# Eight positions modulo 256 bytes for the split-weight buffers of a two-layer decoder trunk

## The chip, the cores and the metric

The kernel runs on one core of one Trainium2 chip. The metric is the device time of one execution in microseconds. Five engines of the core take part: TensorE (PE; its weight loads are shown apart as PEld), VectorE (DVE), ScalarE (ACT), GpSimd (POOL) and SyncE (SP), which here issues DMAs.

## The reference

A sequence of 256 tokens of width 2048 goes through two layers. Layer 0 mixes tokens with a Conformer convolution module, layer 1 with causal stick-breaking attention of 16 heads; each is followed by a gated feed-forward part with 5632 channels and a depthwise convolution of width 3. In short, with all data in float32:

```python
for i in range(2):
    shift, scale, gate = ada_ln(c, mix_mod_w[i], mix_mod_b[i])
    h = rms_norm(x, mix_norm_g[i]) * (1.0 + scale) + shift
    y = conformer_conv_module(h, ...) if i == 0 else stick_breaking_mixer(h, qkv_w, o_w)
    x = x + gate * y
    shift, scale, gate = ada_ln(c, ffn_mod_w[i], ffn_mod_b[i])
    h = rms_norm(x, ffn_norm_g[i]) * (1.0 + scale) + shift
    x = x + gate * conv_ffn(h, up_w[i], dw_w[i], dw_b[i], down_w[i])
return rms_norm(x, final_norm_g)
```

The convolution module is `h @ pw1`, a gate, a causal depthwise convolution of width 31, layer norm, silu, `@ pw2`. `ada_ln` multiplies the conditioning vector by a matrix of 2048 x 6144.

## The kernel before

Activations lie transposed: 128 channels on the partitions, 256 tokens along a row, so that a width of 2048 is 16 tiles. All weights are cut into blocks of 128 x 128 and packed on the host, in the order of use, into pieces of eight blocks (128 x 1024 float32, 4096 bytes in each partition). The order of products is pw1, pw2, then up and down in two halves, q/k/v by groups of heads, o, and up and down again.

The products (all but pw1) are computed with split operands. A piece arrives by DMA in one of six `raw` buffers. ScalarE rounds it to fp32r, which gives `wh` (line 244), and VectorE subtracts, which gives `wl` (line 248). Activations are split in the same way into a hi and a lo tile: `hh`/`hl` after a norm, `zh`/`zl` into pw2, `gh`/`gl` into down, `oh`/`ol` into o. For each block, `gemm` issues a triple of matmuls that add into one PSUM tile:

```python
nc.tensor.matmul(o, wh[:, c], xh[kt], ...)   # L298: hi tile past wh
nc.tensor.matmul(o, wh[:, c], xl[kt], ...)   # L299: lo tile past wh
nc.tensor.matmul(o, wl[:, c], xh[kt], ...)   # L300: hi tile past wl
```

The weight block is loaded into the array and the activation tile of 256 columns moves past it. In the v product (lines 1131 to 1133) the roles are swapped: the activations are the loaded weights, and 512 columns of `wh` or `wl` move. pw1 (line 664) runs in plain float32 on `raw`, without a split. Line 577 multiplies rows of the modulation matrices ("row matmuls"); its data come in the tiles `mrow`, `mraw`, `zrow` and, for three tiles at the end of the convolution, in the split-weight buffers.

Where the tiles lie: the pool `wsplit` has four `wh` and four `wl` buffers of 4096 bytes. 4096 is 16 x 256, so all eight begin at one position modulo 256. Blocks in a piece are 512 bytes apart and keep that position. Tiles of activations take 1056 bytes each (`hh` and `hl` by their 258 columns, the others because `skewed` gives them 8 columns more), and hi and lo alternate, so each begins 32 bytes further on modulo 256 than the one before: hi tiles have four positions, each lo tile is 32 bytes past its hi tile, and the eight positions are all taken.

The convolution of the first stage reads its gated inputs from `u` tiles; tile j lies in buffer j modulo `UBUFS`. A loop over rounds c = 0 to 16 spreads the taps of tile c over rounds c and c + 1. Tiles 0 to 7 are gated up to round 0; tiles 8 to 14 are gated in rounds 2, 4, 6, 8, 9, 11 and 13, and tile 15 in round 14.

The order of instructions on each engine comes from the program's order and, outside some stretches that `in_order` fixes, from a scheduler that looks at readiness and buffers. Engines run their queues strictly in that order. A split of a piece waits until TensorE has done with the piece four before, since that one has the buffers.

Of the kernel before, what the change touches and what calls it, by code (L numbers as in the profile page):

```python
# [10 lines left out]
F32 = mybir.dt.float32  # L11
F32R = mybir.dt.float32r
# [4 lines left out]
P = 128  # L17
PB = 8
PW = PB * P
# [7 lines left out]

SKEW = {"z": (1, 1), "g0": (1, 1), "g1": (1, 1), "o": (1, 1)}
HEAD = 16
UBUFS = 9  # L30
M0 = 6
MORE_ROWS = 4
SPLIT_ROWS = 3
# [84 lines left out]
def hybrid_trunk(ctx: ExitStack, tc: tile.TileContext, cfg: Cfg, io: dict):  # L118
# [7 lines left out]
    xpool = ctx.enter_context(tc.tile_pool(name="xpool", bufs=1))  # L126
    hpool = ctx.enter_context(tc.tile_pool(name="hpool", bufs=1))
    raw_pool = ctx.enter_context(tc.tile_pool(name="raw", bufs=6))
    w_pool = ctx.enter_context(tc.tile_pool(name="wsplit", bufs=4))
    tmp = ctx.enter_context(tc.tile_pool(name="tmp", bufs=2))  # L130
    mpool = ctx.enter_context(tc.tile_pool(name="mpool", bufs=3))
    acc = ctx.enter_context(tc.tile_pool(name="acc", bufs=5, space=PSUM))
# [92 lines left out]
    def load(src, dst):  # L225
        tc.keep_in_program_order(nc.sync.dma_start(dst, src))

    def load_next():
# [4 lines left out]
        load(io["w_" + name][i, :, :n], v[:, :n])  # L233
        raws.append((blocks, v, n))

    def split_next(later=False):

        blocks, v, n = raws[len(parts)]
        if stream[len(parts)][0] == "pw1":
            parts.append((blocks, v, None))  # L240
            return
        wh = w_pool.tile([P, PW], F32R, name="wh")
        wl = w_pool.tile([P, PW], F32R, name="wl")
        nc.scalar.copy(wh[:, :n], v[:, :n])  # L244
        parts.append((blocks, wh, wl))

        def low():
            nc.vector.tensor_tensor(wl[:, :n], v[:, :n], wh[:, :n].bitcast(F32), op=ALU.subtract)  # L248

        if later:  # L250
            return low
        low()
# [243 lines left out]
    with ExitStack() as cv:  # L496
# [39 lines left out]
        def load_rows(most=1):  # L536

            while row_chunks and most:
                n = nrow["n"]
                near = n < nrow["near"]  # L540
                home = row_homes[n] if near else ("zmm"[n % 3] if n < 8 * KD // 4 else "zm"[n % 2]) if "z" in cpar else "m"
                cap = {"m": 3 if near else 1 + (n < 8 * KD // 4), "r": MORE_ROWS, "w": SPLIT_ROWS, "z": 1}[home]
                if sum(t[1] == home for t in row_tiles) >= cap:
                    break
                m, c, k0 = row_chunks.pop(0)
                src = io["mr_" + m][mr_at[m].index(c), :, k0 * 512:(k0 + 4) * 512]
                if home == "w":
                    v = [w_pool.tile([P, PW], F32R, name=x).bitcast(F32) for x in ("wh", "wl")]
                    for i in range(2):
                        load(src[:, i * PW:(i + 1) * PW], v[i])  # L550
                    v = [v[g // 2][:, g % 2 * 512:(g % 2 + 1) * 512] for g in range(4)]
                else:
                    v = (cpool2.tile([P, 4 * 512], F32, name="mrow", bufs=MORE_ROWS) if home == "r" else
                         cpar["z"].tile([P, 4 * 512], F32, name="zrow") if home == "z" else
                         mpool.tile([P, 4 * 512], F32, name="mraw"))
                    if "z" in cpar:
                        nc.gpsimd.dma_start(v, src)
                    else:
                        load(src, v)
                    v = [v[:, g * 512:(g + 1) * 512] for g in range(4)]  # L560
                row_tiles.append((v, home))
                nrow["n"] += 1
                most -= 1
# [80 lines left out]
        PADW = CW - 1  # L644
        us = [cpool2.tile([P, PADW + T], F32, name=f"u{i}") for i in range(UBUFS)]
        for u in us:
# [25 lines left out]
        def gate_mul(j, sg):  # L672
            nc.vector.scalar_tensor_tensor(us[j % UBUFS][:, PADW:], banks.pop(j)[:, :T], pc("pw1_b", j, 1), sg,
                                           op0=ALU.add, op1=ALU.mult)
# [9 lines left out]
        def conv_first(j):  # L684
            if len(conv_banks) < 2:
                conv_banks.append(psum_b())
            conv_ps[j] = conv_banks[j % 2][:, j // 2 % 2 * T:(j // 2 % 2 + 1) * T]
            nc.scalar.activation(conv_ps[j], us[j % UBUFS][:, PADW:], AF.Identity, bias=pc("cdb", j, 1),  # L688
                                 scale=tap(j, PADW))
# [5 lines left out]
        def conv_tensor(j):  # L695

            tens_ps[j] = psum_acc()[:, :T]
            for i in range(LATE_PE):
                k = PADW - LATE_PE + i
                nc.tensor.matmul(tens_ps[j], diag.pop((j, i)), us[j % UBUFS][:, k:k + T], start=i == 0,  # L700
                                 stop=i == LATE_PE - 1)

        def conv_tap(j, k):
            nc.vector.scalar_tensor_tensor(conv_ps[j], us[j % UBUFS][:, k:k + T], tap(j, k), conv_ps[j],  # L704
                                           op0=ALU.mult, op1=ALU.add)
# [3 lines left out]
        def conv_prod(j, i):  # L709
            v = spare.pop(0) if spare else hpool.tile([P, T + 2], F32R, name=f"hl{len(prods) % PRODUCTS}")  # L710
            prods.append(v)
            pr = v[:, :T].bitcast(F32)
            nc.scalar.activation(pr, us[j % UBUFS][:, i:i + T], AF.Copy, scale=tap(j, i))  # L713
            return pr
# [103 lines left out]
        for c in range(KD + 1):  # L818
            late = gates_at.get(c, [])
            squared, squares = [(j, y_square(j)) for j in squares], []  # L820
            if c < M0 + 6:
                load_rows()
            split = lambda j: len(vector_taps(j)) - len(vector_taps(j)) // 2
            taps = [(c, k) for k in vector_taps(c)[:split(c)]] if c < KD else []
            if c > 0:
                old = [(c - 1, k) for k in vector_taps(c - 1)[split(c - 1):]]
                n = max(len(taps), len(old))
                pad = lambda v: v + [None] * (n - len(v))
                taps = [t for pair in zip(pad(taps), pad(old)) for t in pair if t]
            made = 0  # L830
            for s in range(nd):
# [17 lines left out]
                if c == KD and s == 0:  # L849
                    low = split_next(later=True)  # L850
# [322 lines left out]
    for h in range(2):  # L1173
        t = slice(h * HT, (h + 1) * HT)
        nc.vector.reciprocal(rs[:, t], std[:, t])
        v = mpool.tile([P, D], F32, name="mraw")[:, :KD * HT].rearrange("p (k t) -> p k t", k=KD)
# [129 lines left out]
```

## Time and profile before

| | |
|---|---|
| Time, median of 2 runs | 2307.89 us (2307.41 to 2308.37) |
| Span of the profiled execution, first to last instruction | 2304.7 us |
| Mean granted TensorE clock | 0.997 |
| Matmul instructions shown / on lines 298 to 300 | 17834 / 15744 |
| HBM read | 598.58 MB |

The profiled execution's own time is its span and some microseconds around it that no instruction fills; the median of the runs stands 3.2 us above the span. A row of a group in the profile reads: line, engine, operation, tile written <- tiles read, shape, number; then busy time in us, mean ns of one; then the engine's idle time before these. A row of instructions on a tile has the minimum, median and maximum of their durations in ns. A matmul's duration is partly modelled and overlaps the next one's, so its rate is read from how many start in a stretch.

### The profile page before, as it was taken

How to read it: one execution, taken by the hardware profiler on the slowest of the kernel's cores; microseconds unless marked ns; L12 is line 12 of the kernel's file. 1: busy time of each engine (PE TensorE's matmuls, PEld its weight loads, DVE VectorE, ACT ScalarE, POOL GpSimd, SP SyncE). 2: the span in 40 equal slices, each digit the busy share in tenths (PEclk: the TensorE clock that was granted, in tenths of full speed). 3: DMA queues.
4: the chain of work that ended last, by engine and by line, in shares of the span. 5: the costliest groups of instructions: out<-in, count | busy, mean ns of one | idle time of the engine just before them, and what ended most of it. 6: DMA issues, size and time to landing. Idle time of an engine off the chain costs nothing.

```text
span 2304.7 us, 44243 instructions
## 1 busy us (share of the span) xinstructions
PE 2270.8 (99%) x17834; PEld 2168.1 (94%) x17834; DVE 1736.7 (75%) x2386; ACT 1164.4 (51%) x1776; POOL 334.6 (15%) x478
## 2 busy tenths in 40 slices
PE   7999999999999999999999999999999999999997
PEld 5888678999999999999999999999999999999997
DVE  7689968899998899999975555668666545666654
ACT  2056655755543355554465555657555434555443
POOL 4058713200000000002111000121000000000010
PEclk9999999999999999999999999999999999999999
DMA  9988799789999999999854555555555555555553
GB/s 397 417 328 306 272 368 355 272 320 356 358 347 384 363 345 361 355 350 345 304 189 159 165 173 167 172 190 179 190 187 189 187 188 186 190 189 187 190 185 110
DMA packets 139167, 603.56 MB, mean 262 GB/s; under 512 B 15441, under 2 KB 15569, under 8 KB 115153
## 3 DMA queue, kind: packets, MB, share of 16 engines
q1 hardware_dynamic: 120242, 464.42, 56.0%
q0 software_dynamic: 18720, 136.32, 15.8%
q8 instruction: 139, 2.28, 0.4%
q14 instruction: 66, 0.54, 0.1%
HBM read 598.58 MB, written 2.10 MB: 261 GB/s over the span
## 4 chain that ended last, share of the span: by engine, by line
PE 88%; DVE 5%; DMA 4%; ACT 1%; issue 1%; POOL 0%; DVEq 0%; SPq 0%; POOLq 0%; ACTq 0%
PE ps L298 25%; PE ps L299 25%; PE ps L300 25%; PE ps L664 5%; DMA mraw<-in_mt_mix 3%; DVE mraw L331 2%; DVE wl L248 1%; PE ps L1133 1%; PE ps L1131 1%; PE ps L1132 1%; DMA mraw<-in_mt_ffn 1%; PE ps L577 1%; PE auxa L577 1%; DVE hl L382 0%; PE auxb L1132 0%
## 5 line engine op out<-in xcount | busy, mean ns | idle before, releaser
L248 DVE TENSOR_TENSOR wl<-raw,wh 128x1024 fp32r<-128x1024 f32 x688 | 842.9, 1229 | 412.7 <-ACT wh L244 408.0
L244 ACT CAST wh<-raw 128x1024 fp32r<-128x1024 f32 x688 | 719.5, 1048 | 823.9 <-PE ps L299 642.1
L298 PE MATMUL ps<-hh,wh 128*128 128x256 f32 (+1 forms) x3264 | 915.8, 281 | 0.0
L299 PE MATMUL ps<-hl,wh 128*128 128x256 f32 (+1 forms) x3264 | 912.1, 279 | 0.0
L300 PE MATMUL ps<-hh,wl 128*128 128x256 f32 (+1 forms) x3264 | 908.3, 278 | 0.1
L299 PEld LDWEIGHTS ps<-hl,wh 128*128 128x128 f32 x3264 | 617.7, 189 | 0.3
L300 PEld LDWEIGHTS ps<-hh,wl 128*128 128x128 f32 x3264 | 612.8, 188 | 0.7 <-DVE wl L248 0.7
L298 PEld LDWEIGHTS ps<-hh,wh 128*128 128x128 f32 x3264 | 612.7, 188 | 0.3
L299 PE MATMUL ps<-gl,wh 128*128 128x256 f32 x1408 | 396.0, 281 | 0.0
L300 PE MATMUL ps<-gh,wl 128*128 128x256 f32 x1408 | 393.7, 280 | 2.1 <-DVE wl L248 2.1
L298 PE MATMUL ps<-gh,wh 128*128 128x256 f32 x1408 | 394.9, 280 | 0.0
L331 DVE CUSTOM_DVE_ANT_0 mraw<-mraw,csr 128x2048 f32<-128x2048 f32 x152 | 348.2, 2292 | 46.3 <-DMA mraw<-in_mt_mix 30.2
L300 PEld LDWEIGHTS ps<-gh,wl 128*128 128x128 f32 x1408 | 265.5, 189 | 2.3 <-DVE wl L248 2.3
L299 PEld LDWEIGHTS ps<-gl,wh 128*128 128x128 f32 x1408 | 266.5, 189 | 0.0
L298 PEld LDWEIGHTS ps<-gh,wh 128*128 128x128 f32 x1408 | 265.6, 189 | 0.0
L397 POOL TENSOR_TENSOR sumsq<-sumsq,t 128x256 f32<-128x256 f32 x56 | 66.2, 1183 | 879.8 <-ACT t L393 879.5
L664 PE MATMUL ps<-hh,raw 128*128 128x256 f32 x832 | 188.8, 382 | 0.0
L664 PEld LDWEIGHTS ps<-hh,raw 128*128 128x128 f32 x832 | 157.8, 191 | 28.3 <-issue 5.8
L967 DVE SCALAR_TENSOR_TENSOR t<-ps,par,t 128x254 f32<-128x254 f32 x328 | 157.3, 480 | 3.9
L704 DVE SCALAR_TENSOR_TENSOR auxb<-u,cpar,auxb 128x256 f32<-128x256 f32 x297 | 121.6, 483 | 4.5 <-ACT auxb L688 3.7
L839 POOL TENSOR_TENSOR y<-y,hl 128x256 f32<-128x256 f32 x143 | 104.4, 730 | 13.4 <-ACT hl L713 3.3
L964 ACT ACTIVATE t<-ps,par 128x256 f32<-128x256 f32 x164 | 91.9, 560 | 0.0
(247 smaller groups left out, 2270.5 us busy)
## 6 DMA issues: line engine op xcount, KB each, us to landing
raw<-in_w_down SPq DMA_DIRECT2D x176, 512.0 KB, 4.5
mraw<-in_mt_ffn POOLq DMA_DIRECT2D x64, 1024.0 KB, 8.3
raw<-in_w_pw SPq DMA_DIRECT2D x96, 512.0 KB, 8.0
mraw<-in_mt_mix POOLq DMA_DIRECT2D x48, 1024.0 KB, 8.2
raw<-in_w_up01b SPq DMA_DIRECT2D x84, 512.0 KB, 7.0
raw<-in_w_up11b SPq DMA_DIRECT2D x84, 512.0 KB, 3.5
raw<-in_w_up00b SPq DMA_DIRECT2D x80, 512.0 KB, 7.6
raw<-in_w_up10b SPq DMA_DIRECT2D x80, 512.0 KB, 3.5
```

Source lines behind the costliest of these rows:

```text
L244: nc.scalar.copy(wh[:, :n], v[:, :n])
L248: nc.vector.tensor_tensor(wl[:, :n], v[:, :n], wh[:, :n].bitcast(F32), op=ALU.subtract)
L298: nc.tensor.matmul(o, wh[:, c], xh[kt], start=first, stop=False, skip_group_check=halves > 0)
L299: nc.tensor.matmul(o, wh[:, c], xl[kt], start=False, stop=False, skip_group_check=halves > 0)
L300: nc.tensor.matmul(o, wl[:, c], xh[kt], start=False, stop=left[nb] == 0, skip_group_check=halves > 0)
L331: nc.vector.tensor_tensor_reduce(out=v, in0=v, in1=csr, scale=1.0, scalar=0.0, op0=ALU.mult, op1=ALU.add, accum_out=macc[:, nb:nb + 1])
L397: engine.tensor_tensor(self.sum, self.sum, sq, op=ALU.add)
L664: nc.tensor.matmul(banks[j][:, nb // KD * T:(nb // KD + 1) * T], w[:, b * P:(b + 1) * P], hf[kt], start=first, stop=left[j] == 0, skip_gro ...
L704: nc.vector.scalar_tensor_tensor(conv_ps[j], us[j % UBUFS][:, k:k + T], tap(j, k), conv_ps[j], op0=ALU.mult, op1=ALU.add)
L839: nc.gpsimd.tensor_tensor(ys[c], ys[c], pr, op=ALU.add)
L964: nc.scalar.activation(y, ps[:, :T], AF.Identity, bias=pc(f"fdb{i}", nb, 1), scale=w(FW - 1))
L967: nc.vector.scalar_tensor_tensor(y[:, s:], ps[:, :T - s], w(k), y[:, s:], op0=ALU.mult, op1=ALU.add)
```

## The change

The pool `wsplit` now has one buffer for each of eight names, `wh0`, `wl0`, ... `wh3`, `wl3`, and each gets some columns more: by the second number of its pair in `W_PHASES`, eight float32 (32 bytes) each. The first number, an offset in the tile, is 0 everywhere. A counter takes the four pairs in turn, for the splits and for the row tiles as before. The padding is 3, 1, 2, 7, 4, 6, 3 and 0 times 32 bytes in the order wh0, wl0, wh1, ..., so in units of 32 bytes modulo 256 the eight begin at 0, 3, 4, 6, 5, 1, 7 and 2: the `wh` at 0, 4, 5, 7 and the `wl` at 3, 6, 1, 2. The padding is 832 bytes in each partition, and everything allocated behind the pool moves by as much. One `u` buffer of 1152 bytes goes.

```diff
-UBUFS = 9
+UBUFS = 8
+W_PHASES = [((0, 3), (0, 1)), ((0, 2), (0, 7)), ((0, 4), (0, 6)), ((0, 3), (0, 0))]
...
-    w_pool = ctx.enter_context(tc.tile_pool(name="wsplit", bufs=4))
+    w_pool = ctx.enter_context(tc.tile_pool(name="wsplit", bufs=1))
...
+    turn_of = {"w": 0}
+
+    def w_tiles():
+
+        i = turn_of["w"]
+        turn_of["w"] = (i + 1) % len(W_PHASES)
+        return [w_pool.tile([P, PW + 8 * pad], F32R, name=f"{x}{i}")[:, 8 * at:8 * at + PW]
+                for x, (at, pad) in zip(("wh", "wl"), W_PHASES[i])]
+
     def split_next(later=False):
...
-        wh = w_pool.tile([P, PW], F32R, name="wh")
-        wl = w_pool.tile([P, PW], F32R, name="wl")
+        wh, wl = w_tiles()
         nc.scalar.copy(wh[:, :n], v[:, :n])
...
                 if home == "w":
-                    v = [w_pool.tile([P, PW], F32R, name=x).bitcast(F32) for x in ("wh", "wl")]
+                    v = [x.bitcast(F32) for x in w_tiles()]
```

The numbers of instructions stay the same but for one memset of a `u` buffer. Their order changes in a few places, since the scheduler now sees eight names of one buffer and not two of four. The place that the prediction speaks of is the entry of pw2, where layer norm makes the z tiles one by one. On ScalarE, from the first z tile on, there stood before (L925 is the activation that makes z, L378 its hi part, L244 the weight cast):

```order
L378 CAST zh_2259<-t 128x256
L244 CAST wh<-raw 128x1024
L925 ACTIVATE t<-t,cpar 128x256
L378 CAST zh_2271<-t 128x256
L244 CAST wh<-raw 128x1024
L925 ACTIVATE t<-t,cpar 128x256
L378 CAST zh_2283<-t 128x256
L925 ACTIVATE t<-t,cpar 128x256
L378 CAST zh_2291<-t 128x256
L244 CAST wh<-raw 128x1024 x4
```

After, with lines moved by nine, and with a number behind `wh` that rises in the program's order (2293 is the fourth piece of pw2, 2433 the fifth, 2471 the sixth):

```order
L387 CAST zh_2257<-t 128x256
L253 CAST wh_2261<-raw 128x1024
L934 ACTIVATE t<-t,cpar 128x256
L387 CAST zh_2269<-t 128x256
L253 CAST wh_2273<-raw 128x1024
L253 CAST wh_2433<-raw 128x1024
L253 CAST wh_2471<-raw 128x1024
L934 ACTIVATE t<-t,cpar 128x256
L387 CAST zh_2281<-t 128x256
L934 ACTIVATE t<-t,cpar 128x256
L387 CAST zh_2289<-t 128x256
L253 CAST wh_2293<-raw 128x1024
```

The fifth and sixth cast now stand ahead of the third z tile (zh_2281; it was zh_2283), and the fourth behind the fourth z tile as before. On VectorE, between the second and third zl (y and t lead to the next z tile), before:

```order
L379 TENSOR_TENSOR zl_2272<-t,zh_2271 128x256
L599 TENSOR_TENSOR v_mix_98<-auxb,cpar 128x4x4
L522 TENSOR_TENSOR gb<-v_mix_98,cpar 128x16
L248 TENSOR_TENSOR wl<-raw,wh 128x1024
L923 TENSOR_TENSOR y_191<-y_191,dm 128x256
L924 TENSOR_TENSOR t<-y_191,rstd 128x256
L379 TENSOR_TENSOR zl_2284<-t,zh_2283 128x256
```

And after:

```order
L388 TENSOR_TENSOR zl_2270<-t,zh_2269 128x256
L608 TENSOR_TENSOR v_mix_98<-auxb,cpar 128x4x4
L531 TENSOR_TENSOR gb<-v_mix_98,cpar 128x16
L257 TENSOR_TENSOR wl_2274<-raw,wh_2273 128x1024
L932 TENSOR_TENSOR y_191<-y_191,dm 128x256
L257 TENSOR_TENSOR wl_2434<-raw,wh_2433 128x1024
L933 TENSOR_TENSOR t<-y_191,rstd 128x256
L257 TENSOR_TENSOR wl_2472<-raw,wh_2471 128x1024
L388 TENSOR_TENSOR zl_2282<-t,zh_2281 128x256
```

The subtractions of the fifth and sixth piece moved with their casts. On TensorE, at the end of the second piece of pw2 (tile zh_2271), before:

```order
L299 MATMUL ps<-zl_2272,wh 128x256
L300 MATMUL ps<-zh_2271,wl 128x256
L577 MATMUL ps<-mraw,hot 32x512 x4
L298 MATMUL ps<-zh_2283,wh 128x256
L299 MATMUL ps<-zl_2284,wh 128x256
```

And after:

```order
L308 MATMUL ps<-zl_2270,wh_2261 128x256
L309 MATMUL ps<-zh_2269,wl_2262 128x256
L586 MATMUL ps<-mraw,hot 32x512 x8
L307 MATMUL ps<-zh_2281,wh_2273 128x256 x4
L308 MATMUL ps<-zl_2282,wh_2273 128x256
```

Four row matmuls more stand ahead of the third piece; the last of the eight reads the row tile after the next. They are missing further on, between the fifth and the sixth piece. SyncE's queue is unchanged.

## The prediction

> **What bounds the kernel now.** First the page: the busy times and the granted clock.
>
> ```profile
> span 2304.7 us, 44243 instructions
> PE 2270.8 (99%) x17834; PEld 2168.1 (94%) x17834; DVE 1736.7 (75%) x2386; ACT 1164.4 (51%) x1776; POOL 334.6 (15%) x478
> PEclk9999999999999999999999999999999999999999
> ```
>
> TensorE is busy in 99% of the span at an undisturbed clock. Since ends of matmuls are modelled, busy time alone says little, so next I count matmuls in windows by stage (columns: stretch, its length, then busy time and number of instructions of each engine, clock, DMA share, GB/s).
>
> ```profile
> 440.00:1050.00 610.00, 609.60 (x5214) 609.39 (x5213) 575.43 (x710) 302.86 (x410) 50.28 (x95) 1.00 0.94 355
> 1582.00:2290.00 708.00, 708.00 (x6055) 708.00 (x6054) 429.39 (x542) 345.20 (x454) 13.35 (x14) 1.00 0.56 184
> ```
>
> A count takes in the two or three matmuls in flight at an edge (one is shown as 279 ns, and one starts about every 117 ns: 2.4). So the pace, from start to start, is 610.00 / (5214 - 2.4) = 117.05 ns in the first stretch, and 708.00 / (6055 - 2.4) = 116.97 ns in the second. Between them DMA falls from 94% to 56% and VectorE from 94% to 61%, and the pace doesn't move. So neither feeds the limit: it is TensorE's own pace, **117.0 ns a matmul**, and the change is worth what it does to this number. The count comes from the page and from the instructions that touch wl:
>
> ```profile
> L300 PE MATMUL ps<-hh,wl 128*128 128x256 f32 (+1 forms) x3264 | 908.3, 278 | 0.1
> L300 PE MATMUL ps<-gh,wl 128*128 128x256 f32 x1408 | 393.7, 280 | 2.1 <-DVE wl L248 2.1
> L300 PE MATMUL ps<-zh,wl x256: 275/279/292, 286.0 to 407.7; 128*128 128x256 f32 x128
> L300 PE MATMUL ps<-oh,wl x256: 276/278/286, 1455.5 to 1547.8; 128*128 128x256 f32 x128
> L300 PE MATMUL auxb<-hh,wl x32: 276/280/386, 432.2 to 1583.3; 128*128 128x256 f32 x32
> L300 PE MATMUL auxa<-hh,wl x32: 277/279/284, 432.6 to 1584.0; 128*128 128x256 f32 x32
> ```
>
> 3264 + 1408 + 256 + 256 + 32 + 32 = 5248 of L300, and as many of L298 and L299: 15,744. At 117.0 ns that is 1842 us, 80% of the span. One ns of pace is 15.7 us; 2% of the time (46 us), which is about what a measurement of this kernel can tell from no change, would be 2.9 ns.
>
> **The change part by part: positions.** A pass of the plain fp32 product of the first stage (L664) gives the outer bound:
>
> ```profile
> L664 PE MATMUL ps<-hh,raw 128*128 128x256 f32 x141 | 30.6, 379 | 0.0
> ```
>
> These are the 141 in the 30 us from 141 to 171: 30.0 / (141 - 1.8) = 215.5 ns. If an fp32r matmul had half of that (an estimate: 512 columns of it in L1131 below are shown nearly as long as 256 here), it would be 107.8 ns. So 9.2 ns a matmul, 145 us in all, is the most that any placement could bring; and something, not necessarily the placement of weights, costs these 9.2 ns.
>
> What does placement do? The three products below move tiles of other places and in another order past weights that all lie at one place:
>
> ```profile
> 875.00:945.00 70.00, 70.00 (x602) 70.00 (x602) 66.75 (x84) 36.71 (x51) 5.30 (x10) 1.00 0.92 348
> 670.00:730.00 60.00, 60.00 (x512) 60.00 (x512) 53.98 (x55) 22.50 (x22) 5.82 (x11) 1.00 0.99 385
> 1505.00:1530.00 25.00, 25.00 (x217) 25.00 (x216) 17.15 (x19) 12.35 (x18) 6.73 (x5) 1.00 0.57 188
> ```
>
> The up product: 70 / 599.6 = 116.7 ns. Down: 60 / 509.6 = 117.7. The output projection: 25 / 214.6 = 116.5. So 1.2 ns is what such differences make between whole products.
>
> Now count in units of 32 bytes. The moving tiles advance by one unit from hi to lo, so with all weights at one place hi lies at four even distances from them (0, 2, 4, 6) and lo at four odd ones. L298 and L300 (hi) thus meet even distances alone and L299 (lo) odd ones alone. After the change the starts of wh are 0, 4, 5, 7 and of wl 3, 6, 1, 2. Hi then meets wh at even distances in two of four pieces and at odd ones in two; the same holds for lo on wh and hi on wl. Every line will meet all eight distances equally often. Do even and odd differ now?
>
> ```profile
> L298 PE MATMUL ps<-hh,wh 128*128 128x256 f32 x201 | 56.2, 280 | 0.0
> L299 PE MATMUL ps<-hl,wh 128*128 128x256 f32 x201 | 56.1, 279 | 0.0
> L300 PE MATMUL ps<-hh,wl 128*128 128x256 f32 x200 | 55.6, 278 | 0.0
> ```
>
> In the up stretch even gives 280 and 278, odd 279: no difference of parity beyond 1 ns. Mixing them leaves the mean where it is. **This part: 0, between -0.5 and +0.5 ns.**
>
> What is new is that wh and wl no longer begin at the same place, so two of three weight loads in a triple start elsewhere than the one before. The nearest rows are those of the v product, where the weights are the activations (hh, hh, then hl, one unit on):
>
> ```profile
> L1132 PE MATMUL auxb<-wl,hh 128*128 128x512 f32 x32 | 12.7, 396 | 0.0
> L1131 PE MATMUL auxb<-wh,hh 128*128 128x512 f32 x32 | 12.6, 395 | 0.0
> L1133 PE MATMUL auxb<-wh,hl 128*128 128x512 f32 x32 | 12.6, 394 | 0.0
> ```
>
> A change of the weights' place goes with 1 to 2 ns in 512 columns, at most 1 ns in 256. Two of three matmuls: up to 0.7 ns, either way. The two loads that change place (L1133's own and the next L1131's) are the shorter ones, so I take -0.5 ns: 15,744 x 0.5 = **-8 us**. The ends that I keep for the range: the best matmul against the median within one line is 276 to 278 and 274 to 280 in these rows of all distances,
>
> ```profile
> L298 PE MATMUL ps<-oh,wh x256: 274/280/365, 1455.2 to 1547.6; 128*128 128x256 f32 x128
> ```
>
> so -2 ns (-31 us) if the eight places meet mostly good distances; and +1 ns (+16 us), the down product's distance from the up product, if mostly bad ones.
>
> **The moved casts.** The scheduler places the fifth and sixth weight cast of pw2 ahead of the third z tile. The sixth reuses the second piece's buffer, so ScalarE stands until TensorE has finished that piece, with the third z tile queued behind it; on VectorE the wl of both stands ahead of the third zl.
>
> ```profile
> 293.60 0.39 ACT L378 CAST zh<-t 128x256 fp32r<-128x256 f32 x1
> 296.08 3.89 ACT L244 CAST wh<-raw 128x1024 fp32r<-128x1024 f32 x4
> 294.69 0.99 PE ps L577 x8
> 298.76 0.99 PE ps L577 x6
> 290.03 0.53 POOL L557 DMA_DIRECT2D mraw<-in_mr_ffn  x1 [6.93 <-PE ps L577]
> mraw<-in_mr_ffn POOLq DMA_DIRECT2D x11, 1024.0 KB, 8.4
> ```
>
> The second piece ends at 294.7. Cast 1.0, activation 0.6, third zh 0.4: it is there at 296.7, not at 294.0. TensorE's new order puts eight row matmuls (2 us) and not four ahead of the third piece, so it wants the tile at 296.7 too. But the eighth reads a row tile whose load is issued at 290.03 and takes 8.4 us: 298.4. A wait of 2 us, of which 1 us comes back because four row matmuls are then already done: **+1 us, between 0 and +3**. The other moved casts stand at the entries of two products, in these stretches:
>
> ```profile
> 345.00:440.00 95.00, 93.25 (x754) 84.82 (x754) 81.78 (x122) 61.74 (x121) 32.43 (x33) 1.00 0.78 298
> 1553.00:1582.00 29.00, 28.59 (x234) 28.06 (x233) 27.27 (x45) 24.32 (x45) 10.24 (x10) 1.00 0.39 130
> ```
>
> TensorE stands for 1.75 and 0.41 us there today, so a cast that comes one z or hh tile earlier or later can move about 1 us, and I count 0.
>
> **The rest, at nothing.** Eight convolution buffers: tile j now takes that of j-8. The gating of tile 8 is written in round 2 of the convolution loop, and the last reads of tile 0 in round 1; 9 comes in round 4, and so on, and tile 15 in round 14. The buffer is free each time; if it were not, one gating (0.5 us) would wait on VectorE. One small memset goes from the start. All tiles behind the weights move by 832 bytes together and keep their distances. VectorE's subtraction into wl now works on three different places instead of one:
>
> ```profile
> L248 DVE TENSOR_TENSOR wl<-raw,wh 128x1024 fp32r<-128x1024 f32 x25 | 30.4, 1221 | 2.7 <-ACT wh L244 2.5
> ```
>
> VectorE has 70 - 66.75 = 3.25 us to spare in that stretch, 0.13 us for each of the 25; it would have to be a tenth slower to be felt, and nothing shows that.
>
> **Sum.** -8 + 1 + 0 = -7 us on 2304.7; the runs' median stands 3.2 us above the profiled span, so 2307.9 - 7 = **2301 us**.
>
> **The rivals.** *The weights' place does nothing.* For it: loads of weights hardly vary, whatever moves past them, and the rows above show no parity.
>
> ```profile
> L300 PEld LDWEIGHTS ps<-hh,wl x3264: 186/188/195, 407.9 to 2167.3; 128*128 128x128 f32 x192
> ```
>
> Against it: 9.2 ns of unexplained pace. It gives 2308 + 1 = 2309 us. The Trainium skill, "TensorE: Matmul & The Clock Gate", Step-by-step, says the array has two independent read ports, so that loading the next weights takes nothing from the running matmul; by that rule this rival would hold exactly. The loads' 186 to 195 ns agree with it; the 9.2 ns above half of L664's pass are not explained by it.
>
> *Slower: a settled rhythm is broken.* In the up product four triples, one of each distance, take 1.40 us and repeat:
>
> ```profile
> 599.78 0.28 PE L298 MATMUL ps<-hh,wh 128*128 128x256 f32 x1
> 601.18 0.28 PE L298 MATMUL ps<-hh,wh 128*128 128x256 f32 x1
> ```
>
> That is 116.7 ns. With another pair of places every 8 blocks the rhythm must settle again 656 times, and a product such as down, whose tiles come in a less regular order, has 117.7. If all products fall to about 118.3 (that step and half of it more), the price is 1.3 x 15.7 = +20 us: 2328 us. It decides as soon as the pace in the up stretch is above 117.05.
>
> *A large gain.* If most of the spread within a line is contention with one fixed place, the median falls to the best: -3 ns, -47 us, 2261 us. Against it: all four distances already occur, so the best is already averaged in.
>
> **How the numbers follow.** Forecast (2293 to 2305) 0.42; nothing happens (2305 to 2313) 0.27; slower (2313 to 2345) 0.19; large gain (below 2293) 0.12, of which 0.05 below 2262, the bound of 2%. Slower than 2354 has 0.02. The range takes the ends kept above: 2308 - 31 = 2277 below, and 2308 + 16 + 3 = 2327 above. Within 2%: 0.93.
>
> **What the profile after would show.** Windows of 70 us in up products with about 604 matmuls and not 602, means of L298 to L300 lower by half a ns or so, the same for both layers. The moved casts right: a wait of about 2 us on TensorE near 296 to 299. Wrong: a pace that differs by more than 2 ns from 117.0 either way, or by buffers (pieces of one buffer pair quick, of another slow); VectorE slower in L248; or a new wait at a convolution gating.

## The result and the profile after

The changed kernel takes **2324.88 us**, median of 2 runs (2323.68 to 2326.07), against 2307.89 us before: a ratio of 1.0073, with a 95% interval of 1.0056 to 1.0089. It is slower by 17 us, or 0.7%. That is less than the 2% which the prediction took for about what a measurement of this kernel can tell, but the whole interval lies above 1. The forecast was 2301 us; the time lies in the range given (2277 to 2327), with the sign reversed.

First the page after: the span, the busy time of TensorE and the granted clock.

```profile
span 2323.9 us, 44246 instructions
PE 2287.1 (98%) x17834; PEld 2184.4 (94%) x17834; DVE 1736.9 (75%) x2386; ACT 1160.7 (50%) x1776; POOL 329.5 (14%) x477
PEclk9999999999999999999999999999999999999999
```

The span is 19.2 us longer, the number of TensorE's instructions is the same, the clock is the same, and TensorE's busy time has grown by 16.3 us. VectorE, ScalarE and GpSimd have not grown. So it is not a new wait; TensorE itself takes longer for the same work. The same windows as before show the pace (columns: stretch, length, busy time and number for PE, PEld, DVE, ACT, POOL, then clock, DMA share, GB/s):

```profile
440.00:1050.00 610.00, 609.38 (x5160) 609.17 (x5158) 570.28 (x712) 301.90 (x413) 49.21 (x93) 1.00 0.93 352
1582.00:2290.00 708.00, 707.36 (x5989) 707.15 (x5988) 435.32 (x564) 347.84 (x466) 12.80 (x13) 1.00 0.55 187
875.00:945.00 70.00, 70.00 (x595) 70.00 (x594) 65.97 (x84) 35.68 (x49) 5.29 (x10) 1.00 0.93 350
670.00:730.00 60.00, 60.00 (x511) 60.00 (x511) 54.98 (x59) 23.61 (x25) 5.82 (x11) 1.00 0.97 377
1505.00:1530.00 25.00, 25.00 (x214) 25.00 (x213) 17.33 (x18) 12.52 (x20) 6.95 (x5) 1.00 0.53 187
```

610 / (5160 - 2.4) = **118.27 ns** a matmul, and 708 / (5989 - 2.4) = **118.26 ns**; before it was 117.05 and 116.97. The up product in the third row has 595 starts in 70 us where it had 602, so 118.1 and not 116.7; the output projection 118.1 and not 116.5; down, the irregular one, only 118.0 and not 117.7. The products that had been quick lost most. All three lines of the triple have it, and the subtraction into wl has not:

```profile
L307 PE MATMUL ps<-hh,wh 128*128 128x256 f32 (+1 forms) x3264 | 921.2, 282 | 0.0
L308 PE MATMUL ps<-hl,wh 128*128 128x256 f32 (+1 forms) x3264 | 919.0, 282 | 0.0
L309 PE MATMUL ps<-hh,wl 128*128 128x256 f32 (+1 forms) x3264 | 916.3, 281 | 0.1
L257 DVE TENSOR_TENSOR wl<-raw,wh 128x1024 fp32r<-128x1024 f32 x688 | 844.0, 1231 | 423.5 <-ACT wh L253 415.9
```

The last of the three was 278 and is 281. What the regular rhythm of the up product became is seen in the timeline (start in us, duration), one row for every fourth triple:

```profile
1640.11 0.28 PE L307 MATMUL ps<-hh,wh 128*128 128x256 f32 x1
...
1641.53 0.28 PE L307 MATMUL ps<-hh,wh 128*128 128x256 f32 x1
...
1642.95 0.28 PE L307 MATMUL ps<-hh,wh 128*128 128x256 f32 x1
...
1644.37 0.28 PE L307 MATMUL ps<-hh,wh 128*128 128x256 f32 x1
...
1645.81 0.28 PE L307 MATMUL ps<-hh,wh 128*128 128x256 f32 x1
```

Four triples now take 1.42, 1.42, 1.42 and 1.44 us, where they took 1.40 each time. Start times in the trace are finer than these rows; the steps from one start to the next, in ns, read from them in the same up product, show it best. Twelve steps, then the next twelve of the same piece:

```
before, every piece     120 116 116 118 115 116 117 121 112 116 116 117 | the same again       24 steps: 2800
after, pair of buffer 0 117 119 118 118 119 111 120 114 116 117 117 116 | 116 123 113 117 115 120 120 119 112 122 121 118   2818
after, pair of buffer 3 120 120 121 124 117 121 119 113 119 116 120 115 | 119 120 118 118 124 117 119 116 124 117 120 119   2856
```

Before, twelve unequal steps repeat without end and sum to 1400. After, no piece repeats within itself; the four pairs of buffers take 2818, 2822, 2851 and 2856, and that sequence of four pieces repeats.

**Where the 19.2 us of the profiled span lie.** The same matmul, counted from the first, starts later by: 1.4 us at the first of pw2; 2.0 at the 145th (pw2 entered); 3.6 at the first of up (411.4 and not 407.8); 19.5 at the last. So 1.4 us came in the first stage, 0.6 at the entry of pw2, 1.6 in leaving pw2, and 15.9 us in the 14,976 matmuls from there on, 1.06 ns each with all waits. What made the 1.4 us of the first stage is not shown; the kernels below that have the same order of instructions lose 0.0 to 0.6 us there.

### The profile page after: what moved, and what is told of

Read it like the earlier page. It is cut to its first block, busy times and chain, and to the rows that moved or that the text cites. A ratio compares the mean times of both kernels' runs of the same rounds, so it can differ in the third digit from the quotient of the medians.

```text
span 2323.9 us, 44246 instructions
## 1 busy us (share of the span) xinstructions
PE 2287.1 (98%) x17834; PEld 2184.4 (94%) x17834; DVE 1736.9 (75%) x2386; ACT 1160.7 (50%) x1776; POOL 329.5 (14%) x477
## 3 DMA queue, kind: packets, MB, share of 16 engines
q0 software_dynamic: 18720, 136.32, 15.7%
## 4 chain that ended last, share of the span: by engine, by line
PE 90%; DVE 4%; DMA 4%; ACT 1%; issue 1%; POOL 0%; SPq 0%; DVEq 0%; ACTq 0%; POOLq 0%
PE ps L307 26%; PE ps L308 26%; PE ps L309 25%; PE ps L673 5%; DMA mraw<-in_mt_mix 3%; DVE mraw L340 2%; PE ps L1140 1%; PE ps L1141 1%; PE ps L1142 1%; DVE wl L257 1%; PE ps L586 1%; PE auxa L586 1%; DMA mraw<-in_mt_ffn 1%; PE auxb L673 0%; ACT hl L722 0%
## 5 line engine op out<-in xcount | busy, mean ns | idle before, releaser
L257 DVE TENSOR_TENSOR wl<-raw,wh 128x1024 fp32r<-128x1024 f32 x688 | 844.0, 1231 | 423.5 <-ACT wh L253 415.9
L406 POOL TENSOR_TENSOR sumsq<-sumsq,t 128x256 f32<-128x256 f32 x56 | 60.8, 1086 | 889.9 <-ACT t L402 889.6
```

Of the source, the lines that this page charges most:

```text
L406: engine.tensor_tensor(self.sum, self.sum, sq, op=ALU.add)
```

## The experiments

All but the last four of these kernels are the kernel after with another `W_PHASES`: the same eight names, the same order of instructions, the same eight `u` buffers. Places are given in units of 32 bytes modulo 256, counted from where all weights lay before. Where no ratio is given, a kernel ran once beside before. A single time is good to a few us (19 runs of before beside `order_only` lie between 2304.5 and 2309.4); the pace, counted over thousands of matmuls, says more there.

### Order alone, and the place alone

`order_only` takes the padding out, and `one_place` puts it behind the last buffer, so that all weights lie at one place as before and everything behind them is moved by 832 bytes as after.

```diff
-W_PHASES = [((0, 3), (0, 1)), ((0, 2), (0, 7)), ((0, 4), (0, 6)), ((0, 3), (0, 0))]
+W_PHASES = [((0, 0), (0, 0))] * 4                                   # order_only
+W_PHASES = [((0, 0), (0, 0))] * 3 + [((0, 0), (0, 26))]             # one_place
```

> Eight names of one buffer each, without padding: all eight buffers lie at one position modulo 256 as in the kernel before, nothing behind them moves; the order of instructions is that of the change, and there are eight convolution buffers. If the positions cause the 17 us (theory A): pace back at 117.0 ns a matmul, time 2308 to 2312 us. If the new order, or the missing convolution buffer, does (theory B): 2322 to 2326 us with a pace of 117.0 ns and longer waits at the entries of products.

> As the change, with the same 832 bytes of padding, but all of it behind the last buffer: the eight lie at one position, and all that is allocated behind them moves as in the change. Theory A (positions of the weights): 117.0 ns and 2308 to 2313 us. If moving the tiles behind the pool costs (z, g and o tiles by 64 bytes modulo 256, theory C): pace of up unchanged at 116.7 ns, that of down and o higher by 1 ns, 2314 to 2320 us.

`order_only`: 2310.30 us against 2306.13, ratio 1.0016 (1.0007 to 1.0026). `one_place`: 2309.56 us, ratio 1.0015 (1.0006 to 1.0024). Windows of TensorE alone, first `order_only`:

```profile
440.00:1050.00 610.00, 609.35 (x5212) 1.00 0.94 356
1582.00:2290.00 708.00, 707.35 (x6047) 1.00 0.58 184
```

Then `one_place`:

```profile
440.00:1050.00 610.00, 609.35 (x5212) 1.00 0.94 356
1582.00:2290.00 708.00, 707.37 (x6050) 1.00 0.58 184
```

117.1 ns in both, and pieces of 2800 ns in the up products. From 450 to 1050 us the matmuls of `order_only` follow those of before at a constant 3.25 us, without any drift. (Near 1100 us 1.4 us of it come back, by the clock; see the last section.) So the new order, with the eight `u` buffers, costs 3 to 4 us in all, the moved tiles nothing that the intervals could tell, and about 13 us of the 17 belong to the places of the weights. That is shown, not argued: nothing else differs between `one_place` and the kernel after.

### Even distances alone

If odd distances between weights and hi tiles were what costs, pairs at even ones would not pay. `even_0123` puts all wh at 0 and the wl 0, 1, 2 and 3 units behind, one distance to a pair of buffers; `even_4567` the wl 4, 5, 6 and 7 behind. (In these two the names end in letters, by which the trace tells the pairs apart.)

```diff
+W_PHASES = [((0, 0), (0, 0)), ((0, 1), (0, 7)), ((0, 2), (0, 6)), ((0, 3), (0, 7))]   # even_0123
+W_PHASES = [((0, 4), (0, 4)), ((0, 5), (0, 3)), ((0, 6), (0, 2)), ((0, 7), (0, 3))]   # even_4567
```

> All wh at one position, an even number of 32-byte units from the hi tiles as before; the wl of the four pairs 0, 1, 2 and 3 units behind their wh. If the distance from wh to wl costs (theory A1): the pair with 0 keeps 117.0 ns, the others are slower by 0.5 to 2 ns. If only the distance of wh to the hi tiles counts, odd ones being bad (theory A2): all four pairs at 117.0 ns, and 2308 to 2313 us in all.

> As the one before, with the wl 4, 5, 6 and 7 units behind. A1: all four pairs slower than 117.0 ns by 0.5 to 2 ns, about 2320 us in all. A2: all at 117.0 ns.

One run each: 2323.94 and 2321.15 us. The windows of `even_0123`:

```profile
440.00:1050.00 610.00, 609.45 (x5162) 1.00 0.93 352
1582.00:2290.00 708.00, 707.45 (x5992) 1.00 0.58 187
```

118.2 ns. By pair, from the start times: distance 0, 117.9; 1, 118.2; 2, 118.1; 3, 118.3; and in the other kernel 4, 118.5; 5, 117.8; 6, 118.2; 7, 117.7. No distance is quick. The surprise is the first: a pair with the very distances of before, wh on wl, is at 117.9 and not at 117.1. A matmul's time is not its own; it depends on what went ahead.

### Does the change from piece to piece cost, or the layout?

That suggested that a rhythm must settle anew at each piece when the next pair lies elsewhere. `pairs_move` has wl on wh in each pair, and the four pairs at 0, 2, 4 and 6: nothing differs within a piece from before, only from piece to piece. `all_d4` and `all_d1` are the reverse: all wl the same 4 units, or 1, behind all wh, so that nothing changes between pieces. `all_odd` has all eight at place 1.

```diff
+W_PHASES = [((0, 0), (0, 2))] * 3 + [((0, 0), (0, 20))]             # pairs_move
+W_PHASES = [((0, 4), (0, 4))] * 3 + [((0, 4), (0, 6))]              # all_d4
+W_PHASES = [((0, 1), (0, 7))] * 3 + [((0, 1), (0, 1))]              # all_d1
+W_PHASES = [((1, 1), (0, 0)), ..., ((0, 0), (0, 25))]               # all_odd
```

> Each wl at its own wh's position, as in the kernel before; but the four pairs at 0, 2, 4 and 6 units, so that every pair has the kernel before's distances within itself and even ones to the hi tiles. Theory R (TensorE keeps a rhythm that repeats after four blocks as long as the weights stay at one place, and each change of place from piece to piece breaks it): 117.8 to 118.3 ns a matmul, 2320 to 2326 us. Theory D (distances within a triple decide): 117.1 ns, 2308 to 2312 us.

> All wh at one position and all wl at another, 4 units behind: nothing changes from piece to piece. R: the rhythm of four blocks comes back with its own length, the same in each piece, near 117 ns (115.5 to 118). D: this distance had 118.45 ns among mixed pairs, and has it again: about 2327 us.

> As the one before with wl 1 unit behind wh. R: a repeating rhythm near 117 ns. D: 118.2 ns as among mixed pairs, 2323 us.

> All eight at one position, but one unit on: hi tiles now lie at odd distances and lo tiles at even ones. R and the idea that parity does nothing: a repeating rhythm near 117 ns, 2305 to 2315 us. If odd distances of hi are bad (118.5 ns in the two pairs of the change that have them, 117.7 in the others): 118.4 ns, 2326 us.

One run each: 2321.52, 2332.81, 2320.76 and 2324.79 us, beside 2308.14 of before. The windows of `pairs_move`:

```profile
440.00:1050.00 610.00, 609.39 (x5176) 1.00 0.94 353
1582.00:2290.00 708.00, 707.39 (x6008) 1.00 0.59 186
```

And of `all_d4`:

```profile
440.00:1050.00 610.00, 609.49 (x5141) 1.00 0.93 351
1582.00:2290.00 708.00, 707.49 (x5957) 1.00 0.58 186
```

Last of `all_odd`:

```profile
440.00:1050.00 610.00, 609.40 (x5161) 1.00 0.93 352
1582.00:2290.00 708.00, 707.40 (x5990) 1.00 0.59 187
```

`pairs_move` is at 117.9: changing the place between pieces does cost. In its up products one pair of the four falls into the old steps (120 117 116 117 115 116 118 120 113 116 116 116) after four matmuls and takes 2802 ns; the others take 2832 and never reach them. But `all_d4`, where nothing ever changes, is the slowest of all at 118.8, with a repeating pattern that has a step of 131 in it, and `all_d1` and `all_odd` are at 118.2. So the theory that only the change between pieces costs has fallen. `all_odd` differs from `one_place` by one unit in the place of all weights and by nothing else that the products read: hi now meets the odd distances and lo the even ones, and that alone takes the pace from 117.1 to 118.2. Each layout has a repeating pattern of its own, and the one of before is a short one.

### The other distances

`all_two` has all eight weights at place 2, `all_d2` to `all_d7` all wl so many units behind all wh. Two of them, `all_d3` and `all_d6`, ran later, with the kernels of the next part.

```diff
+W_PHASES = [((2, 2), (0, 0)), ..., ((0, 0), (0, 24))]               # all_two
+W_PHASES = [((0, d), (0, 8 - d))] * 3 + [((0, d), (0, ...))]        # all_d2, d3, d5, d6, d7
```

> All eight at one position, 2 units on from the kernel before. The distances to the hi tiles are the same four, met in turned order. Theory P (every layout has a repeating rhythm of its own length, set by the distances alone): 116.7 ns in up and 2308 to 2312 us. Theory M (the rhythm also depends on which position stands where in the order of tiles, so that only the kernel before's very place is good): 118.0 ns, 2322 us.

> As all_d7 with 2 units (118.1 ns among mixed pairs). P: between 116 and 118.5 ns. If equal positions are what is good: 118.0 ns or more.

> As all_d7 with 5 units (117.8 ns among mixed pairs). P: between 115.5 and 118 ns. If equal positions are what is good: 118.0 ns or more.

> All wh at one position as before, all wl 7 units behind. Among mixed pairs this distance had 117.7 ns, less than the pair with distance 0 had there (117.9). P: a rhythm of its own, between 115.5 and 118 ns; below 116.6 ns it would beat the kernel before. If equal positions of wh and wl are what is good: 118.0 ns or more, 2321 us.

> All wh at one place, all wl three units behind. Theory that each layout has a rhythm of its own: a pace between 117.7 and 118.7, as d1, d2, d4, d5 and d7 have, so 2318 to 2333 us. Theory that only wh and wl at one place, at an even distance, keeps the short rhythm: the same, above 117.6. Theory that one distance is quicker than none: below 117.0 and below 2305 us.

> All wh at one place, all wl six units behind. As for three units: 117.7 to 118.7 and 2318 to 2333 us by the theory of a rhythm for each layout; below 117.0 and below 2305 us if this distance is quicker than none.

`all_two`, one run, 2310.44 us (2305.68 before): 117.1 ns and the same steps as before, which is what `order_only` and `one_place` have too. `all_d2`, `all_d5` and `all_d7`, one run each: 2322.28, 2322.48 and 2318.20 us. `all_d3`: 2320.26 us, ratio 1.0060 (1.0045 to 1.0075); `all_d6`: 2321.51 us, ratio 1.0067 (1.0052 to 1.0082), both against 2307.04. Every distance but none is slow, and every one has its own pattern. None of these layouts of the weights beats the one of before.

### The moving tiles, with the weights left alone

So far it could still be the weights alone. Two kernels are **the one before** with eight `u` buffers, its order and its weights, and other places of the activations: `act_even` gives each activation tile 64 bytes more and not 32, so that hi and lo both lie at even distances; `act_flat` takes the 32 bytes from z, g and o, so that all their tiles lie at one place, and leaves h.

```diff
-SKEW = {"z": (1, 1), "g0": (1, 1), "g1": (1, 1), "o": (1, 1)}
+SKEW = {"z": (2, 2), "g0": (2, 2), "g1": (2, 2), "o": (2, 2)}       # act_even, and [P, T + 16] for hh and hl
+SKEW = {"z": (0, 0), "g0": (0, 0), "g1": (0, 0), "o": (0, 0)}       # act_flat
```

> The kernel before with eight u buffers, the weights where they were, and the activation tiles 64 bytes apart and not 32, so that hi and lo both lie at even distances from the weights. Theory that only the weights' places count, and among them the distance between wh and wl: pace 117.05 as before, 2308 us within 3. Theory that the pace belongs to the whole pattern of places, the moving tiles' too: another repeating pattern, a pace outside 116.8 to 117.3, and a time off by 5 us or more; by the observation that the even distances went with the shorter pieces, the pace falls to about 116.5 and the time to about 2300 us.

> The kernel before with eight u buffers, the weights where they were, and the tiles z, g and o without their 32 bytes more, so that each of these products has all its moving tiles at one place; h is as before. Theory that only the weights' places count: the pace of the g products stays at 117.5 and the time at 2308 us within 3. Theory that the whole pattern counts: the pace of g leaves 117.3 to 117.7 while that of h stays at 117.0; g has 4224 matmuls, z and o 768 each, so 1 ns there is 5.8 us; without a change of the moving place I expect the shorter pattern and 2302 us, and 2314 us if moving the tiles on is what helps.

`act_even`: 2325.38 us against 2307.04, ratio 1.0082 (1.0065 to 1.0099). `act_flat`: 2312.38 us, ratio 1.0026 (1.0014 to 1.0038). The windows of `act_even`:

```profile
440.00:1050.00 610.00, 609.66 (x5150) 1.00 0.93 351
1582.00:2290.00 708.00, 707.64 (x5976) 1.00 0.58 187
```

And rows of its timeline, every fourth triple as above:

```profile
1641.30 0.28 PE L298 MATMUL ps<-hh,wh 128*128 128x256 f32 x1
...
1642.72 0.28 PE L298 MATMUL ps<-hh,wh 128*128 128x256 f32 x1
...
1644.14 0.28 PE L298 MATMUL ps<-hh,wh 128*128 128x256 f32 x1
```

118.5 ns, without one weight moved. Its pattern repeats every twelve matmuls as before did (118 119 116 120 112 122 119 119 117 119 117 122), but in 1420 ns and not 1400. My guess that even distances are the good ones was wrong. The windows of `act_flat`, an up product and the down product:

```profile
875.00:945.00 70.00, 70.00 (x602) 1.00 0.93 349
670.00:730.00 60.00, 60.00 (x508) 1.00 0.99 383
```

Up is untouched (602, 116.7 ns); down falls from 512 to 508 matmuls, 60 / 505.6 = 118.7 ns and not 117.7, and the output projection from 217 to 213 in its 25 us. In these two, moving tiles that lie at one place are worse than tiles that move on by 32 bytes. In pw2, which waits break up, no loss shows (steps of 117.7 ns, 118.1 before). The theory that only the weights' places count has fallen.

### The sequence, with every tile left alone

Last, two kernels leave every tile of before where it is and change the order of the three matmuls of a triple.

```diff
 hi past wh
-lo past wh
-hi past wl
+hi past wl
+lo past wh          # lo_last; wl_first: hi past wl, hi past wh, lo past wh
```

> The kernel before with the last two matmuls of each triple exchanged: hi past wh, hi past wl, lo past wh. All tiles lie where they lay. Theory that the sequence of places counts: a repeating pattern other than the 1.40 us of four triples, a pace outside 116.8 to 117.3, the time off by 4 us or more; since 13 of 14 other sequences so far were slower, I expect 117.5 to 118.5 and 2315 to 2331 us. Theory that only the set of places that meet counts: 117.05 and 2308 us within 3, but for wl being wanted one matmul earlier where a piece has just been split.

> As lo_last, with the order hi past wl, hi past wh, lo past wh. The same two theories: 117.5 to 118.5 and 2315 to 2331 us if the sequence counts, 117.05 and 2308 us within 3 if not. wl is made last and is wanted first here, which costs some 1.2 us (one subtraction) at each place where TensorE waits for a fresh piece, a few us in all; the pace in the long stretches is not touched by it.

`lo_last`: 2325.80 us against 2306.54, ratio 1.0086 (1.0071 to 1.0101). `wl_first`: 2323.02 us, ratio 1.0073 (1.0056 to 1.0090). The windows of `lo_last`:

```profile
440.00:1050.00 610.00, 609.68 (x5164) 1.00 0.93 352
1582.00:2290.00 708.00, 707.67 (x5990) 1.00 0.60 187
```

118.2 ns. The same tiles at the same places, and the same pairs of hi, lo, wh and wl, take 1.2 ns more when they follow each other in another order. `wl_first` is at 118.2 too. This settles one more rival, that before is quick because it loads the same block of wh twice running: `wl_first` does so as well, and `lo_last` never does, and the two are alike. Since wl lies at the place of wh here, both pass hi, hi and lo by one place, and in both an up product repeats after 72 matmuls, with pieces of 2833 and 2834 ns. So what counts is the **sequence of places** that TensorE goes through, in weights and moving tiles together. What in the hardware makes the steps unequal is not shown by these runs, and stays open.

### All in one table

Pace by the two windows, as in the prediction.

| kernel | us | pace, 440 to 1050 | pace, 1582 to 2290 |
|---|---|---|---|
| before | 2307.89 | 117.05 | 116.97 |
| order_only, one_place, all_two | 2310.30, 2309.56, 2310.44 | 117.1 | 117.1 |
| act_flat | 2312.38 | 117.29 | 117.48 |
| all_d7 | 2318.20 | 117.72 | 117.73 |
| all_d3, all_d5, pairs_move | 2320.26, 2322.48, 2321.52 | 117.9 | 117.9 |
| all_d6, all_d2, even_4567 | 2321.51, 2322.28, 2321.15 | 118.0 to 118.1 | 118.0 to 118.1 |
| all_d1, even_0123, lo_last, wl_first, all_odd | 2320.76, 2323.94, 2325.80, 2323.02, 2324.79 | 118.2 | 118.2 |
| after | 2324.88 | 118.27 | 118.26 |
| act_even | 2325.38 | 118.50 | 118.52 |
| all_d4 | 2332.81 | 118.71 | 118.90 |

## Why the prediction was wrong, step by step

**What bounds the kernel: right.** TensorE's own pace sets the time. Over the some 15,590 steps from start to start, of the 15,744 matmuls, that no wait and no other matmul stretches (under 140 ns), the mean was 117.17 ns before and 118.11 after; 0.94 x 15.7 = 14.8 us, and with the 3.5 us of the order 18, where 17 were measured. (It is less than the 1.2 ns of the long stretches because down loses 0.4 ns and pw2 nothing.) For the other kernels with this order the same sum comes within 3 us of the time, from `all_d7` (117.69 ns: 12 us, 12.5 measured) to `all_d4` (118.69 ns: 27 us, 24.7 measured), with one exception: for `all_d1` it gives 19 us, and its single run shows 12.6. For `lo_last`, which has the order of before, 0.96 x 15.7 gives 15 us, and 19 were measured.

**The positions: this step failed.** The prediction put them at 0 for parity and -0.5 ns for wl that no longer begins where wh does, -8 us together. They measured +0.94 ns a step, 14.8 us, and about +13 us by the times. Both terms were wrong. Parity alone is `all_odd`: +1.2 ns (118.2 against the 117.1 of `one_place`). A wl apart from its wh, with all wh where they lay, is `all_d1` to `all_d7`: +0.6 ns (`all_d7`) to +1.7 (`all_d4`). At the even distances, which leave parity as it was, it is +0.9 to +1.7 (`all_d6`, `all_d2`, `all_d4`), so this term stands without parity too. The prediction's own sign of being wrong, a pace by buffers, came as well: the up pieces of pairs 0 and 1, whose wh lie at even distances from hi, take 117.4 and 117.6 ns a matmul, and those of pairs 2 and 3, at odd ones, 118.8 and 119.0.

Two readings led there. The first was "mixing them leaves the mean where it is": it took the 280, 279 and 278 ns of the three lines as prices of even and odd distances, each matmul's own. They are not. From start to start, in the products that read h, lines 298 to 300 took 117.9, 117.4 and 115.7 ns before, means over a fixed pattern of steps that repeats. `lo_last`, which changes only the order, has 118.3 for hi past wh, 118.3 for lo past wh and 117.8 for hi past wl. The second was the v product as the nearest row: there the loaded and the moving operand are exchanged, and it said -0.5 ns where all seven distances between wh and wl now gave more. Its sign carried nothing over. The mean over the eight distances, the 117.1 of wl on wh included, is 118.0, so 117.0 was the best of these sequences and not their mean. The kernel after, whose pairs have the distances 3, 2, 4 and 3, lies at 118.3, close to the 118.2 that `all_d3`, `all_d2`, `all_d4` and again `all_d3` average to. That a mixture gets the mean of its parts is not shown by this, since the change from piece to piece costs too (`pairs_move`).

**The lower end of the range, by the best matmul: wrong for the same reason.** "The best matmul against the median" took the spread within a line as good and bad places. The quick steps of 112 and 113 ns are one place in a pattern, paid for by one of 120 or 121 nearby; every layout has them.

**The rival "a settled rhythm is broken": right in size and test, half right in cause.** It gave 118.3 ns and 2328 us, and decided at a pace above 117.05 in the up stretch; 118.1 to 118.3 and 2325 us came out. Its cause was the settling at every change of pair. `pairs_move` shows that this is real (+0.8 ns); the kernels with one distance throughout show that it isn't needed. The row with 1.40 us for four triples had been in the trace. The step from there, that an exactly repeating pattern is one special sequence and that most others should be worse, was priced and then given 0.19. (The chances given add up to 1.02: the four make 1.00 without the 0.02 for times above 2354.)

The loads of weights did not change: a group of the page before, then after.

```profile
L299 PEld LDWEIGHTS ps<-hl,wh 128*128 128x128 f32 x3264 | 617.7, 189 | 0.3
```

```profile
L308 PEld LDWEIGHTS ps<-hl,wh 128*128 128x128 f32 x3264 | 616.8, 189 | 0.3
```

By the Trainium skill, "TensorE: Matmul & The Clock Gate", Step-by-step, TensorE has two independent read ports, and loading the next weights takes no read bandwidth from the running matmul. Loads of 189 ns, unchanged and longer than a step of 117 or 118 ns, agree that they run beside the matmuls; that the pace moves by up to 1.9 ns (`all_d4`) with the places alone does not follow from that rule, and the measurement decides.

**The moved casts: right in the sum, the wait half as long.** The timeline after, at the third piece of pw2:

```profile
296.06 1.05 ACT L253 CAST wh<-raw 128x1024 fp32r<-128x1024 f32 x1 [3.58 <-issue]
...
297.51 0.39 ACT L387 CAST zh<-t 128x256 fp32r<-128x256 f32 x1
297.96 0.14 PEld L586 LDWEIGHTS ps<-mraw,hot 128*32 128x32 f32 x2 [0.94 <-DMA mraw<-in_mr_ffn]
298.94 0.74 PE L307 MATMUL ps<-zh,wh 128*128 128x256 f32 x4
```

ScalarE stands until the second piece is done, casts, and makes the third zh at 297.5; TensorE waits for the row tile's load, as foreseen, though for 0.94 us and not for 2. Counted from the first main matmul, the 73rd starts 1.9 us later than before and the 145th only 0.6 us: +0.6 where +1 was forecast. One profile doesn't fix this: in the 15 kernels with this order it lies between 0.0 (`one_place`) and 2.1 us (`all_d3`), and their mean is 1.0.

**The other moved casts, at 0: wrong by 2 us.** Leaving pw2 costs `order_only` 2.2 us at 350 to 362 us. Most of it is in this profile something that the prediction had no price for, the clock. Windows of TensorE there, `order_only`:

```profile
350.00:354.00 4.00, 2.18 (x19) 1.00 0.84 301
354.00:356.00 2.00, 1.99 (x14) 0.85 0.99 395
356.00:358.00 2.00, 2.00 (x12) 0.50 1.04 438
358.00:360.00 2.00, 2.00 (x15) 0.80 0.41 172
```

And before:

```profile
350.00:354.00 4.00, 2.37 (x20) 1.00 0.97 386
354.00:356.00 2.00, 2.00 (x20) 1.00 1.05 430
356.00:358.00 2.00, 2.00 (x16) 1.00 1.06 393
```

A wait for ScalarE to read out a finished product (`t<-ps`, L942 before and L951 after) grew from 1.91 to 2.12 us between starts, and behind it the granted clock was 0.50 for 3.4 us: 16 matmuls at 213 ns and not 117, which is 1.5 us. The rest is a wait that is 0.4 us longer at 360. But the half clock is not the order's own. It stands between 351 and 367 us in 13 of the 20 traces, among them `act_flat`, `lo_last` and `wl_first`, which have the order of before. And `one_place`, with the new order, kept its full clock there and lost 2.5 us all the same, by waits of 2.54 and 2.59 us between starts where before has 1.91 and 0.65:

```profile
352.00:355.00 3.00, 1.11 (x9) 1.00 0.93 330
358.00:361.00 3.00, 1.49 (x7) 1.00 0.49 208
```

So some 2 us more in leaving pw2 are measured in both; which of the moved instructions makes them is not shown.

**The remainder at nothing: right.** VectorE's subtraction took 1231 ns where it took 1229, on eight places and not on two names. What TensorE waited for, summed over the run after (us, times, longest):

```profile
PE auxb L673 <- ACT hh L649: 11.2, 8, 7.9
PE ps L309 <- DVE wl L257: 3.9, 5, 2.1
PE ps L307 <- ACT t L951: 1.9, 1, 1.9
```

No wait on a convolution gating is among the long ones, and `order_only`, which has eight `u` buffers too, reaches pw2 within 0.01 us of before: eight were enough.

## What to carry to other kernels

When a long stretch of equal instructions repeats exactly, read the steps from start to start and not the mean by line: a mean over positions in a repeating pattern looks like a price of each instruction, and isn't one. A layout that such a pattern rests on (weights at one place, moving tiles 32 bytes on each time, hi, lo, hi) should be kept unless another is measured to be quicker; of the 19 other kernels here the 16 that changed the sequence were all slower, by 0.3% to 1.1%. For a change of layout whose mechanism has no row in the trace, a nearest row with other operands should not set the sign.

## What the runs showed of the hardware that was not expected

- The pace of fp32r matmuls of 256 columns depends on the sequence of start addresses modulo 256 bytes of both operands: 116.7 ns at best (up product before, 2800 ns for 24), 118.9 at worst for a whole layout (`all_d4`, 2853 for 24 in its up products, and 118.90 over the second window). Steps within a pattern run from 111 to 131 ns. Places are told modulo 256 bytes because the pattern of before repeats after four triples, in which the moving tiles go on by 8448 = 33 x 256 bytes, whichever block (512 bytes apart) and buffer (4096) is loaded; a unit of the hardware is not shown by that.
- Moving all eight weights by 64 bytes (`all_two`) leaves the pattern as it was; by 32 bytes (`all_odd`) it gives 118.2 ns. Moving all tiles behind them by 832 bytes (`one_place`) changes nothing; spacing the activations by 64 bytes and not 32 (`act_even`) costs 1.5 ns.
- A stall of TensorE of 2.1 us was followed by 3.4 us at half the granted clock in `order_only`, while one of 1.9 us at the same place before was not, nor two of 2.5 and 2.6 us in `one_place`. The length is that of the window, about 3.4 us, which the Trainium skill, "TensorE: Matmul & The Clock Gate", What's actually happening, gives for the activity monitor. Whether a stall meets it varies between kernels. Behind the long stall near 1100 us it was the other way round, as windows of TensorE show, before:

```profile
1102.00:1104.00 2.00, 2.00 (x12) 0.50 0.97 375
```

And in the same place after:

```profile
1113.00:1115.00 2.00, 2.00 (x20) 1.00 1.01 379
```

So some 1.5 us come or go at such stalls, and a difference of that size between two profiles need not be the edit's own.
